# Attention scores from plain fp32 q and k instead of split halves, in a two-layer decoder trunk

## The chip, the cores and the metric

The kernel runs on one core of one Trainium2 chip. A core has a matrix engine (TensorE; its weight loads are shown as an engine of their own, PEld), VectorE (DVE), ScalarE (ACT), GpSimd (POOL), and queues of transfers that SyncE (SP) issues. They run side by side and wait for each other by semaphores. Matmuls write to PSUM, eight banks of 512 fp32 numbers on each of 128 partitions; everything else lies in SBUF. The metric is the device time of one execution in microseconds (us), smaller being better.

## The reference, cut to what matters

The trunk has two layers. Layer 0 mixes tokens with a gated MLP, layer 1 with dilated window attention; a squared-ReLU MLP follows each. All is fp32. The change lies in the attention, of which this is the core (SEQ = 1024, 16 heads of 64, three patterns of window and dilation):

```python
B_PATTERNS = ((128, 1), (512, 4), (2048, 16))

def dilated_branch(q, k, v, window, dilation, slopes):
    ...
    qb = to_blocks(q)
    kb = with_prev(to_blocks(k))
    vb = with_prev(to_blocks(v))
    s = jnp.einsum('bnqrhe,bnkrhe->bnrhqk', qb, kb,
                   preferred_element_type=jnp.float32) * (E ** -0.5)
    ...
    s = s + bias
    s = jnp.where(valid[None, :, None, None], s, NEG)
    m = jnp.max(s, axis=-1, keepdims=True)
    p = jnp.exp(s - m)
    l = jnp.sum(p, axis=-1, keepdims=True)
    o = jnp.einsum('bnrhqk,bnkrhe->bnqrhe', p / l, vb.astype(jnp.float32))
    lse = (m + jnp.log(l))[..., 0].transpose(0, 1, 4, 2, 3)
    ...

def mixer_b(h, w_qkv, w_out, slopes):
    qkv = (h @ w_qkv).reshape(B, S, N_PAT, 3, B_HEADS, B_HEAD_DIM)
    ...
    wts = jax.nn.softmax(jnp.stack(lses, axis=0), axis=0)[..., None]
    o = jnp.sum(wts * jnp.stack(outs, axis=0), axis=0)
    return o.reshape(B, S, B_HEADS * B_HEAD_DIM).astype(h.dtype) @ w_out
```

## The kernel before

The stages follow one another: gated MLP mixer, MLP, attention, MLP. Most matrix products are made of fp32r numbers, a rounded form of fp32: an operand is split into a rounded part `hi` and the rest `lo` (`split`, lines 100 to 103: ScalarE writes `hi`, VectorE writes `lo = x - hi`), and hi·hi, hi·lo and lo·hi are summed in PSUM.

The attention (`attention`, from line 1047) works through 24 groups: eight pairs of heads, and for each pair the dilations 16, 4 and 1 (`g` = 2, 1, 0). For each group `project` makes q, k and v of both heads: six PSUM banks of 128 rows (two heads of 64) by 512 positions, 24 matmuls of 512 columns each (line 1134). When a bank is full it is emptied with the positions put in the order of the dilation. v is copied by ScalarE (line 1141). q and k are split, for each head e by itself (lines 1143 to 1150):

- `k0`, `k1`: 128 partitions, on the 64 of the head `hi` of k, on the other 64 `lo` of k.
- `q0`, `q1`: `hi` of q on the 64 of the head, and a copy of it, made by GpSimd (line 1150), on the other 64.
- `qlo0`, `qlo1`: `lo` of q on the 64 of the head, zeros on the other 64. These are four tiles that live through the stage, filled with zeros once (line 1064).

So a product of 128 queries with 128 or 256 keys is two fp32r matmuls over all 128 partitions: q hi against k hi and k lo (line 1207), and q lo against k hi (line 1208). The queries are the stationary operand, the keys the moving one. `scores` does two blocks of queries into one PSUM bank; VectorE then adds the bias and takes the extremum (line 1214), ScalarE takes exp and the sum (line 1216). `transposes` turns the weights round on TensorE and splits them, `weighted` multiplies them with v (line 1262), `merge` joins the three dilations.

The order is written out by hand in slots: eight for each group, with three positions each (`at`). In each slot the scores of a later step, the weighted values of an earlier one and the transposes stand between steps of `project`, which runs as a generator beside it and is asked for three matmul triples at a time. So the projection of a later group fills TensorE while the other engines work on the weights of this one. Within an engine a scheduler may move instructions a little. PSUM holds two banks each for scores, weighted values, projections and transposes.

At the end of the stage the output projection starts; its first four accumulators `acc_2_0` to `acc_2_3` take over buffers of `q0`, `q1`, `k0` and `k1` (line 1404).

Of the kernel before, what the change touches and what calls it, by code (L numbers as in the profile page):

```python
# [10 lines left out]
F32 = mybir.dt.float32  # L11
# [6 lines left out]
P = 128  # L18
# [17 lines left out]
def trunk(ctx: ExitStack, tc: tile.TileContext, x, c, ada_w, ada_b, ln_g, ln_b, a_w_in, a_b_in,  # L36
# [6 lines left out]
    def pool(stack, name, bufs, **kw):  # L43
        return stack.enter_context(tc.tile_pool(name=name, bufs=bufs, reuse_waits="tile", **kw))
# [55 lines left out]
    def split(hi, lo, src, hi_engine=A, lo_engine=V):  # L100

        first = A.copy(hi, src) if hi_engine is A else hi_engine.tensor_copy(hi, src)  # L102
        return first, lo_engine.tensor_tensor(lo, src, hi, op=ALU.subtract)  # L103
# [943 lines left out]
    def attention(before):  # L1047
# [6 lines left out]
        with ExitStack() as ph:  # L1054
            open_psum(ph, "B", sc=2, pv=2, mm=2, tr=2)
            vec = pool(ph, "vecB", 1)
            gate = row_tile(gate_dram[2], "gate_2", "gate")
            ql = pool(ph, "attn_qlo", 1)
            qk = pool(ph, "attn_qk", 2)
            qp = pool(ph, "attn", 2)  # L1060
            qlo = [[ql.tile([P, S], F32R, name=f"qlo{e}_{b}") for b in range(2)] for e in range(2)]
            for e in range(2):
                for b in range(2):
                    (V if b else G).memset(qlo[e][b][64 - 64 * e : P - 64 * e, :].bitcast(F32), 0.0)


            near = qp.tile([P, 2 * P], F32, name="near", bufs=1)
            G.iota(near[:], pattern=[[-1, 2 * P]], base=P, channel_multiplier=1, allow_small_or_imprecise_dtypes=True)
# [8 lines left out]
            def perm(t, g, half=None):  # L1077

                d = DILATION[g]
                if g == 0:  # L1080
                    return t if half is None else t[:, half * HALF : (half + 1) * HALF]
                if g == 1:
                    v = t.rearrange("p (r i) -> p r i", r=d)
                    n = v.shape[2] // 2
                else:
                    v = t.rearrange("p (a b i) -> p a b i", b=2, i=S // d)
                    n = v.shape[3] // 2
                return v[..., half * n : (half + 1) * n]

            def by_pos(t, g):  # L1090

                if g == 0:
                    return t
                if g == 1:
                    return t.rearrange("p (i r) -> p r i", r=4)
                return t.rearrange("p (i b a) -> p a b i", b=2, a=8)
# [4 lines left out]
            def project():  # L1101

                todo = [(n, X) for n in range(len(order)) for X in range(3)]
                parts = [(n, X, half) for half in (1, 0) for n, X in todo[:4]]
                parts += [(n, X, half) for n, X in todo[4:] for half in (1, 0)]
                build = before.build(0)

                def load(n, X):
                    hp, g = order[n]
                    c0 = g * 3 * D + X * D + hp * P  # L1110
                    return unit(b_w_qkv[0, :, c0 : c0 + P], f"w{'qkv'[X]}_{hp}_{g}")

                units = {key: load(*key) for key in todo[:4]}
                for n, X, half in parts:
                    if (n, X, half) == (0, 0, 0):
                        run(build)
                    hp, g = order[n]
                    nm = "qkv"[X]
                    i = 3 * n + X
                    if half == 1 and 3 <= i < len(todo) - 1:  # L1120
                        units[todo[i + 1]] = load(*todo[i + 1])
                    if half == 1:
                        if nm == "v":
                            got[n]["vT"] = vec.tile([P, S], F32, name=f"vT_{hp}_{g}", tag="lnb")
                        else:
                            if nm == "q":
                                got[n]["qlo"] = [qlo[e][n % 2] for e in range(2)]
                            for m in ((f"{nm}0", f"{nm}1")):
                                got[n][m] = qk.tile([P, S], F32R, name=f"{m}_{hp}_{g}", tag=m)
                    wu = units[n, X]  # L1130
                    p = bank("mm", f"ps{nm}_{hp}_{g}_{half}")
                    for k in range(KD):
                        for c_, (a, b) in enumerate(((0, 0), (0, 1), (1, 0))):
                            T.matmul(p[:], wu[a][:, k * P : (k + 1) * P], hT[half][b][:, k, :],  # L1134
                                     start=k + c_ == 0, stop=k == KD - 1 and c_ == 2)
                        if half == 1 and (n, X) in ((0, 2), (1, 0)) and k % 2:
                            next(build, None)
                        if k == KD - 1:
                            src = by_pos(p[:], g)
                            if nm == "v":  # L1140
                                A.copy(perm(got[n]["vT"][:], g, half), src)
                            else:
                                for e in range(2):
                                    mine, other = slice(64 * e, 64 * e + 64), slice(64 - 64 * e, P - 64 * e)
                                    t = got[n][f"{nm}{e}"]
                                    hi = perm(t[mine, :], g, half)
                                    lo = perm(got[n]["qlo"][e][mine, :] if nm == "q" else t[other, :], g, half)
                                    split(hi, lo, by_pos(p[mine, :], g))
                                    if nm == "q" and half == 0:
                                        G.tensor_scalar(t[other, :], t[mine, :], 1.0, 1.0, ALU.mult, ALU.mult)  # L1150
                        yield


# [14 lines left out]
            def attend(n, oT_of):  # L1168
# [17 lines left out]
                for e in range(2):  # L1186
# [4 lines left out]
                    def scores(m, e=e, h=h, rows=rows, probs=probs, st=st):  # L1191
                        if m == 0:
                            if e == 0:
                                my["stat"] = qp.tile([P, 2, 2, NT], F32, name=f"stat_{hp}_{g}", tag="stat", bufs=3)
                            st["bias"] = qp.tile([P, width], F32, name=f"bias_{h}_{g}", tag="bias")
                            G.tensor_scalar(st["bias"][:], (far if g == 2 else near)[:],
                                            -8.0 * DILATION[g] * 2.0 ** (-8.0 * (h + 1) / N_HEADS), 1.0, ALU.mult, ALU.mult)
                        scb, used = bank("sc", f"sc_{h}_{g}_{m}"), 0
                        stat = my["stat"]
                        spans = []  # L1200
                        for t in (2 * m, 2 * m + 1):
                            w = 2 * P if has[t] else P
                            sl = slice(used, used + w)
                            used += w
                            k0 = (t - 1) * P if has[t] else t * P
                            tq, keys = slice(t * P, (t + 1) * P), my[f"k{e}"]
                            T.matmul(scb[:, sl], my[f"q{e}"][:, tq], keys[:, k0 : k0 + w], start=True, stop=False)
                            T.matmul(scb[:, sl], my["qlo"][e][:, tq], keys[:, k0 : k0 + w], start=False, stop=True)  # L1208
                            spans.append((t, w, sl))
                        for t, w, sl in spans:  # L1210
                            pr = qp.tile([P, 2 * P], F32, name=f"p_{h}_{g}_{t}", tag="p", bufs=4)
                            col = (t % 2) * 4 + t // 2 if g == 1 else t
                            nm, l = stat[:, 0, e, col : col + 1], stat[:, 1, e, col : col + 1]
                            V.tensor_tensor_reduce(out=pr[:, 0:w], in0=scb[:, sl], in1=st["bias"][:, width - w :], scale=-0.125, scalar=3e38,  # L1214
                                                   op0=ALU.add, op1=ALU.min, accum_out=nm)
                            A.activation(pr[:, 0:w], pr[:, 0:w], AF.Exp, bias=nm, scale=-1.0, accum_out=l)  # L1216
                            probs[t] = pr
# [182 lines left out]
            def output():  # L1400
                box["oT"] = [act_pair(f"oTs_{half}") for half in range(2)]
                res = Residual(2)
                for i in range(4):
                    res.acc[i] = qk.tile([P, D], F32, name=f"acc_2_{i}", tag=("q0", "q1", "k0", "k1")[i])
                out = box["out"] = OutRows(box["oT"], b_w_out[0], gate, res, prepare, "wo")
                for ch in range(2):
                    out.load(ch)
                    prepare(ch)
                box["begin"] = out.begin()
# [56 lines left out]
```

## Time and profile before

| | us |
|---|---|
| runs of the kernel | 2842.47 and 2847.93 |
| median of them | 2845.2 |
| span of the profiled execution, first to last instruction | 2841.6 |

The profile is of one execution. The page gives its span, the two runs beside it their whole time; the median is 3.6 us above the span. Times in the rows are counted from the start of the span; the attention takes about the stretch from 1000 to 2125 us. A row of a group names the line, the engine, the operation, what is written from what, the shape and how many; behind the bar stand the time that they kept the engine busy, the mean length of one in ns, and the idle time of the engine just before them with what ended it. Matmuls overlap in the pipeline of TensorE, so their lengths from start to end add up to more than the time; the distance from start to start is what one costs when they follow closely. A row of the timeline gives start, length, engine, line, and how many like it follow each other.

### The profile page before, as it was taken

To read this page: it belongs to the slowest core of one execution; us is meant where nothing else is said; L and a number is where in the kernel's file an instruction comes from. 1 tells how busy PE (TensorE), PEld (TensorE's weight loads), DVE (VectorE), ACT (ScalarE), POOL (GpSimd) and SP (SyncE) were. 2 spreads that over 40 slices of the span, in tenths; PEclk is the share of its full clock that TensorE was granted. 3 is DMA by queue.
4 is the path that set the end of the run, shared out by engine and by line. 5 is a ranking of instruction groups with operands and counts; after the bars stand their busy time and mean duration, and the time that the engine had idled before them with its cause. 6 is when DMAs were issued, how large, how long until landed. Compare 5 with 4: busy or idle time off the path is not lost.

```text
span 2841.6 us, 36856 instructions
## 1 busy us (share of the span) xinstructions
PE 2752.7 (97%) x13290; PEld 2277.9 (80%) x13290; DVE 1944.5 (68%) x3485; ACT 1413.9 (50%) x2613; POOL 220.1 (8%) x163
## 2 busy tenths in 40 slices
PE   6999999999999999999999999999999999999997
PEld 5777878887888878888888888888877788878886
DVE  6786798777877674656555555555659976577776
ACT  3334375555434455555555555555564755544431
POOL 1021000000000043101000000010201000000000
PEclk9999999999999999999999999999999999999999
DMA  7533346668846343212121212121315564485561
GB/s 253 171 109 106 119 152 223 216 219 277 286 153 201 126 148 105 61 39 68 38 61 39 69 31 69 38 69 31 91 39 178 170 208 158 151 303 189 171 214 60
DMA packets 300186, 384.15 MB, mean 135 GB/s; under 512 B 47532, under 2 KB 172884, under 8 KB 300004
## 3 DMA queue, kind: packets, MB, share of 16 engines
q1 hardware_dynamic: 300004, 381.80, 42.0%
q8 instruction: 104, 1.70, 0.2%
q14 instruction: 78, 0.64, 0.1%
HBM read 297.77 MB, written 83.97 MB: 134 GB/s over the span
## 4 chain that ended last, share of the span: by engine, by line
PE 73%; DVE 11%; DMA 7%; ACT 5%; issue 2%; POOL 2%; SPq 0%; DVEq 0%; ACTq 0%; POOLq 0%
PE psd L938 21%; PE psua L782 10%; PE psv L1134 8%; PE psq L1134 7%; PE psk L1134 5%; PE psuc L782 5%; DMA adaw<-in_ada_w_dram 3%; PE psd_wout L356 3%; PE psub L782 2%; PE pv L1262 2%; PE psd_wo L356 2%; ACT p L1216 1%; DVE adaacc L128 1%; PE psu L356 1%; PE sc L1208 1%
## 5 line engine op out<-in xcount | busy, mean ns | idle before, releaser
L782 PE MATMUL psua<-right,left 128*128 128x512 f32 x1536 | 364.0, 391 | 3.4 <-ACT right L102 1.8
L938 PE MATMUL psd<-rhi,lhi 128*128 128x512 f32 x896 | 351.0, 392 | 2.1 <-ACT part L813 2.1
L938 PE MATMUL psd<-rlo,lhi 128*128 128x512 f32 x896 | 350.9, 392 | 1.2 <-DVE rlo L103 1.1
L938 PE MATMUL psd<-rhi,llo 128*128 128x512 f32 x896 | 350.5, 391 | 0.0
L782 PEld LDWEIGHTS psua<-right,left 128*128 128x128 f32 x1536 | 287.3, 188 | 65.5 <-DVE right L103 3.1
L1216 ACT ACTIVATE p<-p,stat 128x128 f32<-128x128 f32 (+1 forms) x384 | 170.4, 445 | 237.6 <-DVE stat L1214 235.7
L1134 PE MATMUL psv<-hT,wv_hi 128*128 128x512 f32 x768 | 246.0, 401 | 3.2 <-DVE qlo L103 3.2
L1134 PE MATMUL psq<-hT,wq_hi 128*128 128x512 f32 x768 | 246.3, 402 | 0.0
L1134 PE MATMUL psk<-hT,wk_hi 128*128 128x512 f32 x768 | 246.0, 401 | 0.0
L103 DVE TENSOR_TENSOR pTlo<-pT,pThi 128x512 fp32r<-128x512 f32 (+1 forms) x160 | 98.2, 621 | 179.1 <-ACT pThi L102 178.5
L938 PEld LDWEIGHTS psd<-rhi,lhi 128*128 128x128 f32 x896 | 169.3, 189 | 38.4 <-ACT part L813 2.9
L938 PEld LDWEIGHTS psd<-rlo,lhi 128*128 128x128 f32 x896 | 169.1, 189 | 37.0 <-DVE rlo L103 2.2
L938 PEld LDWEIGHTS psd<-rhi,llo 128*128 128x128 f32 x896 | 169.2, 189 | 35.3
L782 PE MATMUL psuc<-right,left 128*128 128x512 f32 x768 | 188.9, 392 | 0.0
L128 DVE SCALAR_TENSOR_TENSOR adaacc<-adaw,silu_c,adaacc 128x512 f32<-128x512 f32 x168 | 133.4, 805 | 64.1 <-DMA adaw<-in_ada_w_dram 63.4
L782 PEld LDWEIGHTS psuc<-right,left 128*128 128x128 f32 x768 | 144.4, 189 | 30.4 <-DVE right L103 0.5
L1214 DVE CUSTOM_DVE_ANT_0 p<-sc,bias 128x128 f32<-128x128 f32 (+1 forms) x384 | 119.7, 347 | 68.6 <-PE sc L1208 66.2
L1134 PEld LDWEIGHTS psv<-hT,wv_hi 128*128 128x128 f32 x768 | 135.6, 189 | 26.1 <-issue 2.8
L1134 PEld LDWEIGHTS psk<-hT,wk_hi 128*128 128x128 f32 x768 | 136.5, 189 | 22.6
L1134 PEld LDWEIGHTS psq<-hT,wq_hi 128*128 128x128 f32 x768 | 135.7, 189 | 22.2
L1134 PE MATMUL psq<-hT,wq_lo 128*128 128x512 f32 x384 | 151.4, 394 | 0.0
L1134 PE MATMUL psv<-hT,wv_lo 128*128 128x512 f32 x384 | 150.6, 392 | 0.0
(250 smaller groups left out, 5843.1 us busy)
## 6 DMA issues: line engine op xcount, KB each, us to landing
lraw<-forms SPq DMA_DIRECT2D x112, 512.0 KB, 3.7
adaw<-in_ada_w_dram SPq DMA_DIRECT2D x192, 256.0 KB, 3.2
up<-in_mlp_w_up_dram SPq DMA_DIRECT2D x64, 512.0 KB, 3.8
forms<-s SPq DMA_DIRECT2D x128, 256.0 KB, 2.4
rraw<-in_mlp_w_down_dram SPq DMA_DIRECT2D x64, 512.0 KB, 4.5
forms<-part SPq DMA_DIRECT2D x96, 256.0 KB, 2.5
spill<-acc SPq DMA_DIRECT2D x24, 512.0 KB, 2.7
wq_raw<-in_b_w_qkv_dram SPq DMA_DIRECT2D x24, 512.0 KB, 3.7
```

What stands on the lines that cost most here:

```text
L103: return first, lo_engine.tensor_tensor(lo, src, hi, op=ALU.subtract)
L128: ins = V.scalar_tensor_tensor(acc[:], raw[:], silu_c[:, k : k + 1], acc[:], ALU.mult, ALU.add)
L356: T.matmul(dst, s[a], m[b], start=(n == 0), stop=(n == last))
L782: T.matmul(acc, w[:, a, k, :], right[p][:, b, k, :], start=p in (1, 2, 5) and k + a + b == 0, stop=k == 3 and a == 1, skip_group_check=True)
L938: T.matmul(sums[kind, m][:], l[a][:, k, m * P : (m + 1) * P], r[b][:, k, :], start=p in (1, 5, 2, 3) and kp + k + a + b == 0, stop=kp == K ...
L1134: T.matmul(p[:], wu[a][:, k * P : (k + 1) * P], hT[half][b][:, k, :], start=k + c_ == 0, stop=k == KD - 1 and c_ == 2)
L1208: T.matmul(scb[:, sl], my["qlo"][e][:, tq], keys[:, k0 : k0 + w], start=False, stop=True)
L1214: V.tensor_tensor_reduce(out=pr[:, 0:w], in0=scb[:, sl], in1=st["bias"][:, width - w :], scale=-0.125, scalar=3e38, op0=ALU.add, op1=ALU.m ...
L1216: A.activation(pr[:, 0:w], pr[:, 0:w], AF.Exp, bias=nm, scale=-1.0, accum_out=l)
L1262: T.matmul(pvs[b][:, q0 % HALF : q0 % HALF + w_], stt, x_[:, o_ : o_ + w_], start=not begun[b], stop=left[b] == 0, skip_group_check=True)
```

## The change

q and k of a group are each kept once, as plain fp32, both heads in one tile of 128 partitions. q is copied out of PSUM by ScalarE, k by VectorE, one instruction for each bank of 512 positions. The score of a block is a single fp32 matmul over the 64 partitions of its head. The split of q and k, the copy on GpSimd and the four `qlo` tiles with their memsets go away, and the four accumulators of the output projection get buffers of their own.

```diff
@@ -1055,14 +1055,8 @@
-            ql = pool(ph, "attn_qlo", 1)
+            qp = pool(ph, "attn", 2)
             qk = pool(ph, "attn_qk", 2)
-            qp = pool(ph, "attn", 2)
-            qlo = [[ql.tile([P, S], F32R, name=f"qlo{e}_{b}") for b in range(2)] for e in range(2)]
-            for e in range(2):
-                for b in range(2):
-                    (V if b else G).memset(qlo[e][b][64 - 64 * e : P - 64 * e, :].bitcast(F32), 0.0)
@@ -1123,10 +1117,7 @@
-                            if nm == "q":
-                                got[n]["qlo"] = [qlo[e][n % 2] for e in range(2)]
-                            for m in ((f"{nm}0", f"{nm}1")):
-                                got[n][m] = qk.tile([P, S], F32R, name=f"{m}_{hp}_{g}", tag=m)
+                            got[n][nm] = qk.tile([P, S], F32, name=f"{nm}_{hp}_{g}", tag=nm)
@@ -1140,14 +1131,11 @@
                             if nm == "v":
                                 A.copy(perm(got[n]["vT"][:], g, half), src)
                             else:
-                                for e in range(2):
-                                    mine, other = slice(64 * e, 64 * e + 64), slice(64 - 64 * e, P - 64 * e)
-                                    t = got[n][f"{nm}{e}"]
-                                    hi = perm(t[mine, :], g, half)
-                                    lo = perm(got[n]["qlo"][e][mine, :] if nm == "q" else t[other, :], g, half)
-                                    split(hi, lo, by_pos(p[mine, :], g))
-                                    if nm == "q" and half == 0:
-                                        G.tensor_scalar(t[other, :], t[mine, :], 1.0, 1.0, ALU.mult, ALU.mult)
+                                dst = perm(got[n][nm][:], g, half)
+                                if nm == "q":
+                                    A.copy(dst, src)
+                                else:
+                                    V.tensor_copy(dst, src)
@@ -1203,9 +1191,8 @@
-                            tq, keys = slice(t * P, (t + 1) * P), my[f"k{e}"]
-                            T.matmul(scb[:, sl], my[f"q{e}"][:, tq], keys[:, k0 : k0 + w], start=True, stop=False)
-                            T.matmul(scb[:, sl], my["qlo"][e][:, tq], keys[:, k0 : k0 + w], start=False, stop=True)
+                            T.matmul(scb[:, sl], my["q"][rows, t * P : (t + 1) * P], my["k"][rows, k0 : k0 + w],
+                                     start=True, stop=True)
@@ -1401,7 +1388,7 @@
-                    res.acc[i] = qk.tile([P, D], F32, name=f"acc_2_{i}", tag=("q0", "q1", "k0", "k1")[i])
+                    res.acc[i] = qk.tile([P, D], F32, name=f"acc_2_{i}", tag=f"acc{i}", bufs=1)
```

The order on TensorE, first block of scores of a group with dilation 4 in the fifth pair of heads, before; `psq` is a projection bank, `sc` the scores, `pv` the weighted values, and the last number of a name is that of its buffer:

```order
L1134 MATMUL psq_0_1_14178<-hT_1_0_8086,wq_0_lo 128x512
L1207 MATMUL sc_1_0_14232<-k_4_1_13919,q_4_1_13737 128x128
L1208 MATMUL sc_1_0_14232<-k_4_1_13919,qlo_1_8453 128x128
L1207 MATMUL sc_1_0_14232<-k_4_1_13919,q_4_1_13737 128x256
L1208 MATMUL sc_1_0_14232<-k_4_1_13919,qlo_1_8453 128x256
L1262 MATMUL pv_2_1_14148<-pThi_2_1_14210,v_2_13847 128x128
```

The same place with the change (line numbers are those of the changed file):

```order
L1125 MATMUL psq_0_1_13736<-hT_1_0_8086,wq_0_lo 128x512
L1194 MATMUL sc_1_0_13785<-k_1_13495,q_1_13328 128x128
L1194 MATMUL sc_1_0_13785<-k_1_13495,q_1_13328 128x256
L1249 MATMUL pv_2_1_13707<-pThi_2_1_13766,v_2_13430 128x128
L1249 MATMUL pv_2_1_13707<-pTlo_2_1_13767,v_2_13430 128x128
```

Each pair has become one matmul at the same place; what stands ahead and behind is the same, here and nearly everywhere on this engine.

The order on VectorE where the k of that group leaves PSUM, before (`L1214` is the reduction of the scores, `L1347` and `L1350` belong to the merge of the three dilations):

```order
L103 TENSOR_TENSOR k_4_1_13919<-psk_1_0_13990,k_4_1_13919 64x4x128
L1214 ISA p_2_0_14051,stat_2_13807<-sc_2_0_14046,bias_2_14044 128x128
L1214 ISA stat_2_13807 128x1
L1214 ISA p_2_1_14054,stat_2_13807<-sc_2_0_14046,bias_2_14044 128x128
L1214 ISA stat_2_13807 128x1
L1280 TENSOR_TENSOR oT_2_14065<-oT_2_14065,pv_2_0_13963 64x4x2x64
L103 TENSOR_TENSOR k_4_1_13920<-psk_1_0_13990,k_4_1_13920 64x4x128
```

And with the change:

```order
L1138 COPY k_1_13495<-psk_1_0_13560 128x4x128
L1334 TENSOR_TENSOR oT_0_13216<-oT_0_13216,bc_0_13506 128x1024
L1201 ISA p_2_0_13614,stat_2_13392<-sc_2_0_13611,bias_2_13609 128x128
L1201 ISA stat_2_13392 128x1
L1337 TENSOR_TENSOR oT_0_13216<-oT_0_13216,oT_1_12832 128x1024
L1201 ISA p_2_1_13617,stat_2_13392<-sc_2_0_13611,bias_2_13609 128x128
```

One copy stands for two subtractions, with no wait for ScalarE between them, and a scaling and a sum of the merge have slid in among the reductions of the scores, where before they stood ahead of them.

## The prediction

> **What bounds the kernel now.** I read the page first: the busy times, the 40 slices, and the chain of work that ended last.
>
> ```profile
> span 2841.6 us, 36856 instructions
> PE 2752.7 (97%) x13290; PEld 2277.9 (80%) x13290; DVE 1944.5 (68%) x3485; ACT 1413.9 (50%) x2613; POOL 220.1 (8%) x163
> PE   6999999999999999999999999999999999999997
> PEclk9999999999999999999999999999999999999999
> PE 73%; DVE 11%; DMA 7%; ACT 5%; issue 2%; POOL 2%; SPq 0%; DVEq 0%; ACTq 0%; POOLq 0%
> ```
>
> TensorE carries the kernel: 97% busy, 9 tenths or more in every slice but the first and the last, and 73% of the chain. Its granted clock is flat, so the clock is no part of the answer. The change touches the attention stage alone. The table of windows gives its steady part, seven pairs of heads of 136 us each (columns: PE, PEld, DVE, ACT, POOL busy, then clock and DMA):
>
> ```profile
> 1100.00:2052.00 952.00, 941.10 (x5070) 791.01 (x5069) 532.41 (x1291) 513.20 (x1219) 105.51 (x98) 1.00 0.21 55
> ```
>
> TensorE is busy 941 of 952 us; VectorE has 44% of the stage free, ScalarE 46%. So a microsecond of TensorE issue added here is a microsecond of the kernel, and one taken from VectorE, ScalarE or GpSimd is worth only what TensorE waits for them. What TensorE waited for between 1000 and 2125 us (total, times, longest):
>
> ```profile
> PE pv L1262 <- DVE pTlo L103: 4.1, 10, 0.5
> PE pT L1239 <- DVE v L103: 3.6, 8, 0.5
> PE psv L1134 <- DVE qlo L103: 3.2, 2, 2.4
> PE pT L1239 <- ACT p L1216: 2.7, 10, 0.6
> PE pT L1242 <- ACT p L1216: 1.6, 7, 0.4
> ```
>
> That is 15.2 us, all that relief of the other engines could give back.
>
> **What the scores cost now.** The groups by shape:
>
> ```profile
> L1208 PE MATMUL sc<-k,qlo 128*128 128x128 f32 x208 | 54.0, 275 | 0.0
> L1207 PE MATMUL sc<-k,q 128*128 128x256 f32 x176 | 51.7, 306 | 0.1
> L1208 PE MATMUL sc<-k,qlo 128*128 128x256 f32 x176 | 47.7, 282 | 0.0
> L1207 PE MATMUL sc<-k,q 128*128 128x128 f32 x208 | 46.8, 241 | 0.0
> ```
>
> So 384 products, 208 with 128 keys and 176 with 256, two matmuls each. The means are from start to end and overlap, so they are no price; the price is from start to start, and the timeline of TensorE has it. First one block with a product of each width, between projection matmuls and the weighted values, then one block with two wide products, then one with two narrow ones:
>
> ```profile
> 1514.07 0.62 PE L1134 MATMUL psk<-hT,wk_hi 128*128 128x512 f32 x2
> 1514.52 0.39 PE L1134 MATMUL psk<-hT,wk_lo 128*128 128x512 f32 x1
> 1514.75 0.22 PE L1207 MATMUL sc<-k,q 128*128 128x128 f32 x1
> 1514.81 0.28 PE L1208 MATMUL sc<-k,qlo 128*128 128x128 f32 x1
> ...
> 1515.21 0.28 PE L1262 MATMUL pv<-pThi,v 128*128 128x256 f32 x1
> ...
> 1548.08 0.28 PE L1207 MATMUL sc<-k,q 128*128 128x256 f32 x1
> ...
> 1548.55 0.40 PE L1134 MATMUL psq<-hT,wq_hi 128*128 128x512 f32 x1
> ...
> 1593.79 0.22 PE L1207 MATMUL sc<-k,q 128*128 128x128 f32 x1
> ...
> 1594.18 0.45 PE L1134 MATMUL psq<-hT,wq_hi 128*128 128x512 f32 x1
> ```
>
> A mixed block takes 0.46 us (1515.21 less 1514.75), a wide one 0.47, a narrow one 0.39. Per head the code makes 4 narrow blocks (dilation 16), 4 mixed ones (dilation 4), and one mixed and three wide ones (dilation 1): over 16 heads 64 narrow, 80 mixed, 48 wide. Now: 64 x 0.39 + 80 x 0.46 + 48 x 0.47 = 25.0 + 36.8 + 22.6 = 84.4 us. The first two rows give the other price: three matmuls of 512 columns take 0.68 us (1514.07 to 1514.75), 0.227 each, or 0.44 ns for a column, when the weight load runs under the matmul before it. That wide and narrow blocks cost nearly the same shows that short matmuls are set by something else, the weight loads, which follow each other at 0.11 us:
>
> ```profile
> 1508.99 0.19 PEld L1208 LDWEIGHTS sc<-k,qlo 128*128 128x128 f32 x1
> 1509.10 0.19 PEld L1207 LDWEIGHTS sc<-k,q 128*128 128x128 f32 x1
> ```
>
> **The change on TensorE.** The order of its instructions stays; each pair becomes one fp32 matmul over 64 rows. No matmul in this trace multiplies plain fp32 (the fp32 ones are transposes), so its price is bounded from the rows. Lower end: it streams once like one short matmul of now, half the pairs' price, 42 us for all, a gain of 42. Upper end: it streams once for each of the four products of halves, and two weight loads (high and low half of q) lie bare each time. In between: four streams with the loads hidden, 4 x 128 = 512 or 4 x 256 = 1024 columns, hence 0.227 or 0.454 us by the row of 512 columns. I take this value. The kernel of now shows why one stream is unlikely: it splits both operands and spends 128 rows to get three of the four half-products in two streams; 64 rows leave no second half of the array to lay a product in, and unrounded operands need all four. And it is nearest to the rows where a load had 0.11 us or more of matmul to hide under: each half of such a product is a stream of at least 256 columns, 0.114 us against 0.11. Sum: 208 x 0.227 + 176 x 0.454 = 47.2 + 79.9 = 127.1 us, less 84.4: **plus 43 us**. Nearly all of it comes from the wide products; a narrow block goes from 0.39 to 0.45.
>
> The Trainium skill, FP8 and Floating Point Precision, TensorE Precision Notes, states that true FP32 takes four passes through the array; by it the sum is the same 127 us if loads stay hidden, and no run here shows it yet.
>
> **The change on the other engines.** Removed and added copies out of PSUM (the last row, a plain VectorE copy of this size in the first stage, prices the new k copy; vT prices the new q copy):
>
> ```profile
> L102 ACT CAST k<-psk 64x512 fp32r<-64x512 f32 x96 | 55.7, 580 | 38.6 <-DVE k L103 21.5 <-PE psk L1134 15.4
> L102 ACT CAST q<-psq 64x512 fp32r<-64x512 f32 x96 | 55.6, 579 | 70.0 <-DVE qlo L103 36.4 <-PE psq L1134 33.2
> L1141 ACT COPY vT<-psv 128x512 f32<-128x512 f32 x48 | 28.0, 584 | 4.6 <-PE psv L1134 4.2
> L103 DVE TENSOR_TENSOR k<-psk,k 64x512 fp32r<-64x512 f32 x96 | 66.1, 689 | 36.0 <-ACT k L102 32.8
> L103 DVE TENSOR_TENSOR qlo<-psq,q 64x512 fp32r<-64x512 f32 x96 | 66.0, 687 | 40.0 <-ACT q L102 38.0
> L1150 POOL TENSOR_SCALAR q<-q 64x1024 fp32r<-64x1024 f32 x48 | 61.1, 1273 | 295.7 <-ACT q L102 295.2
> L462 DVE COPY vz<-psvt x16: 674/685/692, 62.7 to 149.5; 128x512 f32<-128x512 f32 x16
> ```
>
> ScalarE: less 111.3, plus 48 x 0.584 = 28.0, so 83 us less. VectorE: less 132.1, plus 48 x 0.685 = 32.9, so 99 us less. GpSimd: 61 us less, and of the four memsets two each go from VectorE and GpSimd. All of this lay under TensorE and is worth nothing by itself. On the path are the waits above. The 3.2 us are the start of the stage, where the third projection needs a PSUM bank that four steps on two engines empty; one copy empties it now, and I take 3 us. Of the other 12.0 us, waits on the queues of VectorE and ScalarE, which get about a seventh shorter, I take 5; the bounds are 0 and 12. What is late next there is the same chain of exp, transpose and split, so not all of it goes. The accumulators of the output projection get buffers of their own; no row of that stage shows a wait for the old ones, so it is worth nothing. No DMA is added or moved.
>
> **Sum.** Plus 43, less 8: plus 35 us on a span of 2841.6, 2876.6. The median of the runs, 2845.2, is 3.6 above this span, so I say 2880, 1.2% slower. About 2% (57 us) is what a measurement of this kernel can tell from no change, so this counts as the same.
>
> **Rivals.**
> *TensorE runs empty at each change of array shape* (ends as slower). Score blocks use 64 rows, all around them 128. If a change of shape lets the array run dry, each costs what is still in flight when the next matmul would start: 0.39 long, 0.227 spaced, so 0.16 us; 192 blocks x 2 x 0.16 = 61 us, 2941. It decides from 0.06 us a change (22 us to the 2% line, over 384). Against it speaks the one other shape in the trace, the transposed statistics on 128*32:
>
> ```profile
> 1180.91 0.39 PE L1134 MATMUL psq<-hT,wq_lo 128*128 128x512 f32 x1
> 1181.14 0.27 PE L1294 MATMUL pstat<-ident,stat 128*32 128x128 f32 x1
> 1181.17 0.31 PE L1207 MATMUL sc<-k,q 128*128 128x128 f32 x1
> 1181.31 0.27 PE L1208 MATMUL sc<-k,qlo 128*128 128x128 f32 x1
> ```
>
> It enters 0.23 us after a 512-column matmul, as any other, and two matmuls later only 0.17 us have gone by. That changes columns, not rows, so the rival keeps 15%. The Trainium skill, TensorEngine Tiling, Key Properties, has the rule that changing the tiling mode drains TensorE; by it the time is the 2941 above, and these four rows do not agree with it for columns.
>
> *The weight loads of an fp32 matmul lie bare* (slower). If the second half of q can't be loaded while the first is in use, two loads a product show at the 0.11 us of the rows: 384 x 2 x 0.11 = 84 us, 2964; one load, 42 us, 2922. For it: short matmuls are already set by loads. Against it: loads do run under the matmul before everywhere here. 25%.
>
> *The fp32 matmul is cheaper than four streams.* Two streams with loads as now: 2837 with the waits gained; one stream: 2795; with all 15 us of waits gone, 2788, the only way to a gain of 2%. 6%.
>
> *A new wait takes the old one's place.* q now leaves PSUM by ScalarE alone and k by VectorE alone, and VectorE's order lets a sum of the merge of the three dilations fall between two score reductions:
>
> ```profile
> L1350 DVE TENSOR_TENSOR oT<-oT,oT 128x1024 f32<-128x1024 f32 x14 | 18.7, 1335 | 0.7
> ```
>
> Seven merges at 1.3 us: 9 us, 2889. It lies in the likeliest case's own range.
>
> **How the numbers follow.** Four hidden streams 54%, own range 2860 to 2902; empty array 15%; bare loads 25%, to 2964; cheaper 6%. The predicted time is that of the first. The range reaches down to 2848 (three streams instead of four: 127.1 x 3/4 = 95, so plus 11, less 8) and up to 2965, the two bare loads; outside it lie the cheap cases and both slow ones together. Faster by over 2%: 3%. Slower by over 2%: the 40% of the two slow rivals and a little of the first case's edge, 41%. Within: 56%.
>
> **What would show it.** Right: a mixed block about 0.68 us from start to start (0.227 + 0.454), a wide one 0.91, a narrow one 0.45; the wait of psv at the start of the stage gone; ScalarE some 83 and VectorE some 99 us less busy; TensorE still about 99% busy from 1100 us on, each pair of heads some 5 us longer. An empty array shows as 0.16 us more both ahead of the first score and behind the last of a block. Bare loads show as gaps inside a block, narrow blocks at 0.8 us or more. My sum is wrong if the narrow blocks grow as much as the wide ones, or if TensorE's idle time grows.

## The result and the profile after

| | us |
|---|---|
| before, median of 2 runs | 2845.2 |
| after, runs | 2923.99 and 2926.82 |
| after, median | 2925.4 |
| ratio, with its 95% interval | 1.0287 [1.0265, 1.0309] |
| span of the profiled execution after | 2922.3 |

The changed kernel is 2.9% slower: 80 us, where the prediction had plus 35. That is the forecast direction with more than twice its size. The span grew by 80.7 us, and the granted clock stayed flat. The page after, busy times and the chain of work that ended last:

```profile
span 2922.3 us, 36435 instructions
PE 2848.4 (97%) x13290; PEld 2282.3 (78%) x13290; DVE 1844.3 (63%) x3339; ACT 1334.8 (46%) x2469; POOL 155.1 (5%) x113
...
PE 85%; DVE 8%; DMA 3%; issue 1%; ACT 1%; POOL 0%; SPq 0%; DVEq 0%; POOLq 0%; ACTq 0%
```

VectorE fell by 100 us, ScalarE by 79, GpSimd by 65, and TensorE's share of the chain rose from 73% to 85%: it now waits for hardly anyone. The count of its instructions did not change although 768 matmuls of the scores became 384 in the code: each plain fp32 matmul is two records here. The table of windows for about the same seven pairs of heads (length, then PE, PEld, DVE, ACT, POOL busy, clock, DMA):

```profile
1100.00:2134.00 1034.00, 1034.00 (x5113) 800.83 (x5112) 449.43 (x1174) 448.40 (x1105) 52.12 (x55) 1.00 0.19 52
```

This window holds 43 matmul records more than the one before (5113, before 5070); from the same projection matmul to the same one, these pairs take 1027 us instead of 953, 10.5 us more for each pair where the prediction had some 5. TensorE is busy in all of it. This is the row that misleads. A matmul counts as busy from its start to its modelled end, so a stretch in which the last one only runs out of the pipeline counts too. Idle time on TensorE fell by 15 us over the span (88.9 to 73.9) while the kernel lost 80.

The groups by shape show where to look (busy time, mean ns, then the idle time before them and what ended it):

```profile
L1194 PE MATMUL sc<-k,q 64*128 64x256 f32 x352 | 102.5, 392 | 0.0
L1194 PE MATMUL sc<-k,q 64*128 64x128 f32 x416 | 84.2, 307 | 0.0
...
L1194 PEld LDWEIGHTS sc<-k,q 64*128 64x128 f32 x768 | 106.3, 186 | 70.5 <-issue 67.1 <-DVE pTlo L103 0.4
...
L1249 PEld LDWEIGHTS pv<-pThi,v 128*128 128x128 f32 x400 | 74.2, 188 | 40.2 <-issue 30.5 <-ACT q L1136 5.0 <-ACT pThi L102 0.5
```

The matmuls stand idle for nothing, but their weight loads stand idle 67.1 us ahead of scores and 30.5 us ahead of weighted values, for "issue", that is, for no other engine. The waits of the weight loads in the attention stage count them (total, times, longest):

```profile
PEld sc L1194 <- issue: 67.1, 190, 0.4
PEld pv L1249 <- issue: 30.5, 92, 0.3
```

There are 190 such waits ahead of scores, about one for each of the 195 uninterrupted stretches of score matmuls (nearly always one block), each 0.35 us. One block with a product of each width in the timeline of TensorE (start, length, then how many like it; a row of several prints the shape of the first), and the loads of the same moment:

```profile
1605.06 0.62 PE L1125 MATMUL psk<-hT,wk_hi 128*128 128x512 f32 x2
1605.52 0.39 PE L1125 MATMUL psk<-hT,wk_lo 128*128 128x512 f32 x1
1605.84 0.92 PE L1194 MATMUL sc<-k,q 64*128 64x128 f32 x4
1606.68 0.39 PE L1249 MATMUL pv<-pThi,v 128*128 128x256 f32 x1
1606.91 0.28 PE L1249 MATMUL pv<-pTlo,v 128*128 128x256 f32 x1
```

```profile
1605.29 0.19 PEld L1125 LDWEIGHTS psk<-hT,wk_lo 128*128 128x128 f32 x1
1605.83 0.52 PEld L1194 LDWEIGHTS sc<-k,q 64*128 64x128 f32 x4 [0.35 <-issue]
1606.68 0.19 PEld L1249 LDWEIGHTS pv<-pThi,v 128*128 128x128 f32 x1 [0.33 <-issue]
1606.79 0.19 PEld L1249 LDWEIGHTS pv<-pTlo,v 128*128 128x128 f32 x1
```

Between full-row matmuls, a load starts together with the matmul ahead of its own (the load of 1605.29 is for the matmul of 1605.52, and runs under the second of the two that begin at 1605.06). The first load of the scores starts at 1605.83, with its own matmul, and so does the first load behind them, at 1606.68. From the last projection matmul to the first score are 0.32 us instead of 0.23, and the block takes 0.84 us from start to start where 0.68 was forecast. Both edges of the block are late; nothing inside it is.

What TensorE still waits for, 1000 to 2205 us (total, times, longest), against the 15.2 us before:

```profile
PE psvt L1170 <- ACT vT L1132: 3.8, 1, 3.8
PE pv L1249 <- DVE pTlo L103: 1.0, 2, 0.5
PE psd_wo L356 <- ACT acc L374: 0.5, 1, 0.5
PE pstat L1281 <- DVE pTlo L103: 0.3, 1, 0.3
```

The wait of psv at the start of the stage is gone, and so are the short ones for ScalarE's p and VectorE's v; those for pTlo fell to 1.0 us. One of 3.8 us for the copy of vT is new.

### The profile page after: what moved, and what is told of

Same layout as the page of the kernel before. It is cut to its first block, busy times and chain, and to the rows that moved or that the text cites. A ratio compares the mean times of both kernels' runs of the same rounds, so it can differ in the third digit from the quotient of the medians.

```text
span 2922.3 us, 36435 instructions
## 1 busy us (share of the span) xinstructions
PE 2848.4 (97%) x13290; PEld 2282.3 (78%) x13290; DVE 1844.3 (63%) x3339; ACT 1334.8 (46%) x2469; POOL 155.1 (5%) x113
## 4 chain that ended last, share of the span: by engine, by line
PE 85%; DVE 8%; DMA 3%; issue 1%; ACT 1%; POOL 0%; SPq 0%; DVEq 0%; POOLq 0%; ACTq 0%
PE psd L938 20%; PE psua L782 10%; PE psk L1125 9%; PE psv L1125 9%; PE psq L1125 9%; PE sc L1194 5%; PE psuc L782 5%; PE pv L1249 4%; PE psd_wout L356 3%; PE psub L782 3%; PE psu L356 2%; DMA adaw<-in_ada_w_dram 2%; PE psd_wo L356 2%; PE pT L1226 1%; DVE adaacc L128 1%
## 5 line engine op out<-in xcount | busy, mean ns | idle before, releaser
L1194 PE MATMUL sc<-k,q 64*128 64x128 f32 (+1 forms) x768 | 173.8, 346 | 0.0
L1194 PEld LDWEIGHTS sc<-k,q 64*128 64x128 f32 x768 | 106.3, 186 | 70.5 <-issue 67.1
```

Source lines behind the costliest of these rows:

```text
L1194: T.matmul(scb[:, sl], my["q"][rows, t * P : (t + 1) * P], my["k"][rows, k0 : k0 + w], start=True, stop=True)
```

## The experiments

The theories on record: A, that the change between matmuls over 64 and over 128 rows lets the array run dry at both edges of a block; B, that the change between rounded and plain fp32 does it; and for the relief of the other engines, C, that it is worth 28 us, against 8 to 15. Four of the experiments (128 rows in plain fp32, 64 rows rounded, half the edges, the relief) were run beside one set of runs of the kernel before (median 2845.2), the other two beside another (2842.7). In the diffs "..." stands for other lines of the same change.

**Plain fp32 over 128 rows.** The queries of each head lie in a tile of their own with zeros in the other head's 64 rows, so that type, passes and order stay and only the rows change.

```diff
...
-                                    A.copy(dst, src)
+                                    for e in range(2):
+                                        mine = slice(64 * e, 64 * e + 64)
+                                        A.copy(perm(got[n][nm][e][mine, :], g, half), by_pos(p[mine, :], g))
...
-                            T.matmul(scb[:, sl], my["q"][rows, t * P : (t + 1) * P], my["k"][rows, k0 : k0 + w],
+                            T.matmul(scb[:, sl], my["q"][e][:, t * P : (t + 1) * P], my["k"][:, k0 : k0 + w],
```

> Plain fp32 as in the change, but over all 128 rows: q of each head stands alone on its 64 rows with zeros on the other 64, k holds both heads. Same number of fp32 streams, no change between 64 and 128 rows. Theory A (a change of the number of rows lets the array run dry, about 0.19 us each, some 390 times, 75 us): the weight load ahead of a score block starts under the matmul before it again, a block of two products of different width takes about 0.66 us instead of 0.85, and the time is about 2858 us (2845, plus 38 for the streams, less 25 for the shorter queues of VectorE and ScalarE). Theory B (the switch between fp32r and plain fp32 costs it, whatever the rows): blocks as in the change, about 2925 us.

It took 2866.1 us (4 runs), ratio 1.0083 [1.0067, 1.01] to the kernel before, 59 us less than the changed kernel, and 8 us more than theory A expected, which had 25 us for the relief. A block with a product of each width in its timeline, and the group of its weight loads:

```profile
1539.62 0.39 PE L1130 MATMUL psv<-hT,wv_lo 128*128 128x512 f32 x1
1539.85 0.81 PE L1200 MATMUL sc<-k,qz 128*128 128x128 f32 x4
1540.31 0.47 PE L1255 MATMUL pv<-pThi,v 128*128 128x256 f32 x1
1540.62 0.28 PE L1255 MATMUL pv<-pTlo,v 128*128 128x256 f32 x1
```

```profile
L1200 PEld LDWEIGHTS sc<-k,qz 128*128 128x128 f32 x768 | 121.3, 189 | 18.0
```

The first score comes 0.23 us after the projection matmul again, and the loads wait for no issue. From that projection matmul to the second matmul of weighted values are 1.00 us (1539.62 to 1540.62), against 1.39 with 64 rows (1605.52 to 1606.91): 0.39 us for one entry and one exit. Rounded and plain matmuls alternate here just as in the changed kernel and cost nothing at the edges, so B falls. Inside a block a pass takes the same time over 128 rows as over 64, 0.11 us for 128 columns and 0.22 for 256, from the end of one to the end of the next.

**Rounded fp32 over 64 rows, one pass.** The changed kernel with the tiles of q and k rounded: no change of type at the edge of a block, but the change of rows.

```diff
-                            got[n][nm] = qk.tile([P, S], F32, name=f"{nm}_{hp}_{g}", tag=nm)
+                            got[n][nm] = qk.tile([P, S], F32R, name=f"{nm}_{hp}_{g}", tag=nm)
```

> q and k kept as fp32r, so one pass for a product; the low halves of q and k are left out of the scores. Rows as in the change: 64. Theory A: the 0.19 us on both sides of every block stay, the streams shrink from 123 to about 43 us: about 2847 us. Theory B: no such gaps, since all is fp32r: about 2772 us.

It took 2849.4 us (one run): with half the score matmuls of the kernel before it is no faster. The weight loads have the same waits as in the changed kernel, without any plain fp32 in the scores (first row). The timeline of a block with two narrow products follows:

```profile
PEld sc L1194 <- issue: 66.3, 188, 0.4
```

```profile
1611.91 0.39 PE L1125 MATMUL psk<-hT,wk_lo 128*128 128x512 f32 x1
1612.22 0.44 PE L1194 MATMUL sc<-k,q 64*128 64x128 f32 x2
1612.59 0.73 PE L1125 MATMUL psk<-hT,wk_hi 128*128 128x512 f32 x2
1613.15 0.39 PE L1125 MATMUL psk<-hT,wk_lo 128*128 128x512 f32 x1
```

**Rounded fp32 over 128 rows, one pass.** The kernel of the first experiment, with its two kinds of tiles rounded: the partner of the run above.

```diff
...
-            qz = [[ql.tile([P, S], F32, name=f"qz{e}_{b}") for b in range(2)] for e in range(2)]
+            qz = [[ql.tile([P, S], F32R, name=f"qz{e}_{b}") for b in range(2)] for e in range(2)]
...
-                            got[n][nm] = [qz[e][n % 2] for e in range(2)] if nm == "q" else qk.tile([P, S], F32, name=f"{nm}_{hp}_{g}", tag=nm)
+                            got[n][nm] = [qz[e][n % 2] for e in range(2)] if nm == "q" else qk.tile([P, S], F32R, name=f"{nm}_{hp}_{g}", tag=nm)
```

> The fourth corner of rows and type: q and k as fp32r, one pass for a product, over all 128 rows with zeros on the 64 of the other head. The low halves of q and k are left out of the scores, as in the run over 64 rows. Theory A (the number of rows makes the gaps): no gaps, 384 short matmuls at 0.11 to 0.12 us, 43 us instead of the 85 of before, and some 10 us from the shorter queues: about 2793 us, 56 less than with 64 rows. If the gaps had another cause than the rows, they stay: about 2849 us.

It took 2801.9 us, ratio 0.985 [0.9835, 0.9865], 47 us less than over 64 rows. The same kind of block:

```profile
1596.65 0.39 PE L1130 MATMUL psv<-hT,wv_lo 128*128 128x512 f32 x1
1596.88 0.33 PE L1200 MATMUL sc<-k,qz 128*128 128x128 f32 x2
1597.05 0.68 PE L1130 MATMUL psv<-hT,wv_hi 128*128 128x512 f32 x2
1597.57 0.39 PE L1130 MATMUL psv<-hT,wv_lo 128*128 128x512 f32 x1
```

From one low-half projection matmul to the next are 0.92 us, with 64 rows 1.24: 0.32 us for the two edges. In this pair the scores have the rounded type of the matmuls around them, and only the rows differ on TensorE (ScalarE copies q twice, 64 rows at a time, instead of once). The whole kernel gained 9 us less than theory A expected. With it go the waits of the weight loads for the exponentials, which are longer when TensorE gets faster: 22.0 us in the two rows below, 9.6 in the run over 64 rows (5.6 and 4.0). That these waits are the whole of the 9 us is not shown.

```profile
PEld pT L1235 <- ACT p L1209: 11.4, 29, 1.0
PEld pT L1232 <- ACT p L1209: 10.6, 17, 1.1
```

The four kernels side by side, in us:

| scores | 64 rows | 128 rows | rows alone |
|---|---|---|---|
| plain fp32, four products of halves | 2925.4 | 2866.1 | 59 |
| rounded fp32, one product | 2849.4 | 2801.9 | 47 |

The two kernels of the last row stand beside different runs of the kernel before; each taken against its own, the difference is 45 us.

**Half as many edges.** The changed kernel with the score blocks of a head issued two at a time: as many matmuls over 64 rows, in about 100 stretches instead of 195.

```diff
-                        at(base + 4 * e + m, 0)(lambda m=m, f=scores: f(m))
+                        at(base + 4 * e + m // 2 * 2, 0)(lambda m=m, f=scores: f(m))
```

> As the change, but the scores of two blocks are issued together in every other slot, so that there are about 100 stretches of score matmuls instead of 195. Theory A and B alike (a fixed cost at entry and exit): 95 x 2 x 0.19 = 36 us less, about 2889 us, perhaps some us more for later scores. If the gaps came with each matmul or each block instead: about 2925 us.

It took 2891.5 us (one run), 34 us less than the changed kernel. The waits of the weight loads ahead of scores halved with the edges, and each stayed as long:

```profile
PEld sc L1194 <- issue: 33.5, 95, 0.4
```

So the price belongs to the edge, not to a matmul over 64 rows: 34 us over 95 stretches fewer is 0.36 us for each stretch, which has two edges.

**The relief alone.** Two matmuls over 128 rows for each product as before, in rounded fp32, but with the changed kernel's single copies of q and k.

```diff
...
-                            T.matmul(scb[:, sl], my["q"][rows, t * P : (t + 1) * P], my["k"][rows, k0 : k0 + w],
-                                     start=True, stop=True)
+                            for c_ in range(2):
+                                T.matmul(scb[:, sl], my["q"][:, t * P : (t + 1) * P], my["k"][:, k0 : k0 + w],
+                                         start=c_ == 0, stop=c_ == 1)
```

> TensorE does what it did before the change, two fp32r matmuls over 128 rows for a product, 768 in all; q and k leave PSUM as in the change, by one copy each (rounded; the low halves and the separation of the heads are left out of the scores). So only the work of VectorE, ScalarE and GpSimd shrinks. Theory C (shorter queues are worth some 28 us, since every wait of TensorE also costs the 0.16 us of the matmul in flight, which the table of waits does not count): about 2817 us. Rival (they are worth the 8 us of the prediction, 15 at most): 2830 to 2837 us.

It took 2832.5 us (4 runs), ratio 0.9956 [0.9941, 0.9971]: the relief is worth 13 us, and theory C falls. What TensorE waited for in the stage, against the 15.2 us before:

```profile
PE psd_wo L356 <- DVE acc L376: 4.6, 3, 3.2
PE pT L1227 <- ACT p L1204: 2.6, 3, 2.1
PE pv L1250 <- DVE pTlo L103: 2.0, 4, 1.1
PE pT L1230 <- ACT p L1204: 1.9, 4, 1.2
```

The waits of pT for v and of psv for qlo are gone, the other three fell from 8.4 to 6.5 us; the first row belongs to the output projection behind the attention. The empty time recovered there is 8.7 us (15.2 less 6.5; a new wait of psvt for vT takes 1.1 of it back), less than the gain. The rest seems to lie at the weight loads, whose lateness need not leave TensorE empty. Their waits in the kernel before, and then in this run:

```profile
PEld pT L1242 <- ACT p L1216: 9.6, 22, 0.7
PEld pv L1262 <- DVE pTlo L103: 9.2, 19, 0.7
PEld pT L1239 <- ACT p L1216: 8.4, 22, 0.8
PEld pT L1239 <- DVE v L103: 7.0, 8, 1.0
```

```profile
PEld pT L1230 <- ACT p L1204: 9.9, 26, 1.3
...
PEld pT L1227 <- ACT p L1204: 4.5, 6, 2.5
PEld pv L1250 <- DVE pTlo L103: 3.3, 7, 1.3
PEld pT L1227 <- DVE v L103: 1.9, 8, 0.2
```

In these four kinds they fell from 34.2 us to 19.6, by 14.6, which is close to what the kernel gained; that one makes up the other is argued from the sizes, not shown.

**Plain fp32 over 128 rows for dilation 16 alone.** There all products are narrow, and with the matmul behind it a narrow block of two plain products over 128 rows had cost as much as the rounded pairs of before (medians end to end: 0.444 + 0.231 us, before 0.395 + 0.281). The groups with dilations 1 and 4 keep the halves of the kernel before.

```diff
...
+                            if g == 2:
+                                T.matmul(scb[:, sl], my[f"q{e}"][:, tq], my["k0"][:, k0 : k0 + w], start=True, stop=True)
+                                spans.append((t, w, sl))
+                                continue
```

> The kernel before, with plain fp32 over 128 rows (q padded with zeros, one copy of k) in the groups of dilation 16 alone, where all products are 128 wide; the whole score is computed. TensorE pays 64 blocks x 0.05 us (0.448 for four streams against 0.395) = 3.5 us. If a third of the 13 us that the shorter queues gave comes back, and 2 us at the start of the stage: about 2841 us, 0.1% under before. If the queues of the other two groups are what counts: about 2848 us.

It took 2835.5 us (6 runs), ratio 0.9966 [0.9952, 0.9979]: 0.3% faster than the kernel before, under both times expected, and the fastest of these with the whole score computed. The prediction took 2% as the least that can be told from no change; with this many runs the interval is 0.14% on either side.

```profile
L1217 PE MATMUL sc<-k,q 128*128 128x128 f32 x256 | 38.8, 274 | 0.0
```

The 128 narrow products of this dilation are 256 passes, each weight load again under the matmul ahead of it. Scores take 88.5 us in the stage, counted from end to end (before: 85.3), while the first matmuls behind a block (29.3, before 32.3), the weighted values (76.9, before 81.0), the projections and the transposes give back more.

## Why the prediction missed

Matmuls overlap, so I summed distances from the end of one to the end of the next over all matmuls of the attention stage, each booked to the later one; the rows then add up to the stage, in us. The ends are modelled, so single distances are rough; the sums are held by the runs above. Start to start, which the text ahead of the prediction uses, misleads here: over 128 rows the mixed block of plain fp32 shown above has 0.46 us from its start to the next start (1539.85 to 1540.31), but 0.65 from end to end, since the matmul behind it starts early and lasts longer.

| booked to | before | relief alone | fp32, 128 rows | after |
|---|---|---|---|---|
| scores, entry included | 85.3 | 85.3 | 122.4 | 160.2 |
| first matmul behind a block | 32.3 | 32.2 | 29.0 | 65.7 |
| transposes pT | 81.3 | 72.1 | 72.8 | 63.4 |
| weighted values pv | 81.0 | 75.6 | 76.0 | 71.9 |
| psvt | 21.0 | 22.3 | 22.0 | 25.8 |
| projections of q, k, v | 794.1 | 792.0 | 793.2 | 791.9 |
| rest | 26.5 | 26.6 | 26.5 | 26.6 |
| stage | 1121.5 | 1106.1 | 1141.9 | 1205.5 |

**Four streams: right, a little mis-sized.** Fp32 over 128 rows differs from before in the streams: plus 37.1 (122.4 less 85.3), forecast plus 43. One pass of 256 columns, which carries two of the four streams, takes 0.216 us end to end, where the forecast had 0.227; one of 128 columns 0.112, forecast 0.114. The rival of a cheaper matmul falls, and so does that of bare loads: inside a block passes follow at these distances with no gap. With one bare load a product that rival gave 2922 us, the number nearest to the 2925 measured; that is chance.

**"It is nearest to the rows where a load had 0.11 us or more of matmul to hide under": right inside a block, wrong at its edges.** This is the step that failed: the forecast put the edges of a block at nothing. The first load of a block often had a 512-column matmul to hide under and did not use it, because that matmul ran over 128 rows and the load's own over 64. The prediction had this as its rival of the array that runs empty, at 15%, 0.16 us a change and 2941 us in all. The measured price: against fp32 over 128 rows, entries cost 37.8 us more (160.2 less 122.4) and exits 36.7 (65.7 less 29.0), together 74.5 over 2 x 195 edges, 0.19 us each. The rounded pair gives 0.18 by the same sum. An entry costs as much more for a first pass of either width, in the medians from end to end: 0.303 us against 0.109 for 128 columns, 0.410 against 0.216 for 256. That these 74.5 us are more than the 59 between the two kernels is taken up below. The rival's 2941 is only 16 us from the measured time, partly by luck: its edges were 13 us too cheap, while its streams and its relief, and waits that it did not know of, were off the other way.

The argument that held the rival down was the transposed statistics on 128*32, which pass without a gap. They change columns. It was said that this is not rows, yet the chance followed the row that was at hand. The rule of the Trainium skill, TensorEngine Tiling, Key Properties, that a change of tiling mode drains TensorE, agrees with these runs for a change of rows, and the 128*32 rows of the kernel before still do not show it for a change of columns. The Trainium skill, TensorE: Matmul & The Clock Gate, Single matmul latency, puts the drain of a single bf16 matmul at about 175 ns; the 0.19 us here, with rounded and plain fp32, is near it, which does not make them the same thing. The runs do not separate how much of the 0.19 is the array running dry and how much is the load that starts late.

**The relief: right mechanism, the term too small.** Forecast 8 us, within 15.2. Alone it was worth 13 us in the medians and 15 in the stage of the profiled execution, nearly all at pT (9.2) and pv (5.4). In the stage that is the whole of the bound. The bound was a sum of the time in which TensorE was empty, and the lateness of weight loads, 34.2 us before, is not all in it. The forecast for the engines' busy times held: ScalarE 79 us less for 83, VectorE 100 for 99, GpSimd 65 for 61.

**What the prediction had no term for: the lost time pays some waits.** The prediction took a microsecond added on TensorE as a microsecond of the kernel. From fp32 over 128 rows to the changed kernel the stage grows by 63.6 us, not by 74.5, since pT (9.4), pv (4.1) and the projections (1.3) give time back, while psvt takes 3.8 more with its new wait. The reading is that the exponentials catch up while TensorE stands at the edges. In the sum: 37.1 for streams, less 16.7 for relief and cheaper exits of that kernel, plus 74.5 for edges, less 10.9 for waits that they hide: 84.0 in the stage, 80 in the time. That this last part is hidden waiting is read from the table; that it is not a trait of plain fp32 is supported by the rounded pair, whose 68.7 us of edges became 47 of time.

**The other rivals and signs.** The merge's sum between the reductions, 9 us, showed as no wait of TensorE. A narrow block took 0.64 us (median, start to what follows) for a forecast 0.45, a wide one 1.06 for 0.91: both are over by about as much, 0.19 and 0.15, as a fixed price for each block makes them. The sign against the sum, narrow blocks growing as much as wide ones, did not show all the same: they grew by 0.24 us and the wide ones by 0.58, since the streams of the wide ones grew too. The sign of the empty array, 0.16 us more at both edges, did. Two signs were badly chosen: TensorE's idle time did not grow, and its 99% came out as 100%, with 74.5 us lost at the edges in the stage. The Trainium skill, Perfetto Trace Analysis, says at its head that matmul busy time judges a kernel badly because matmuls are pipelined; the window with 1034.00 busy of 1034.00 agrees.

## What to carry to other kernels

Before a matmul is cut from 128 to 64 rows, count how often it meets full-row matmuls in the order on TensorE and price each edge, 0.19 us here; here zeros in the unused rows avoided it, and issuing two blocks together halved it. Judge matmuls by distances from end to end and by the waits of their weight loads, for "busy" counts a pipeline running out as work. And a table of waits shows only empty time: the relief behind it can be worth as much as the whole table or more, and a new loss on the bounding engine can cost less than its own sum, when other waits disappear into it.

## What was not expected of the hardware

- A plain fp32 matmul shows as two LDWEIGHTS and two MATMUL records, 0.112 us a pass for 128 columns and 0.216 for 256. Over 128 rows and for 128 keys it cost no more than two rounded matmuls (0.68 us in the median, from end to end, for a block with two narrow products and the matmul behind it, in both).
- A change of rows between 64 and 128 cost about 0.19 us in each direction here, whether the type changes with it or not. Whether two groups of 64 rows that lie in different halves of the array cost it among themselves was not tried.
